# Weight splits of the A/B projections, issued two column blocks ahead and in front of the modulation steps

## The chip, the cores and the metric

The kernel runs on one core of a Trainium2 chip. A core has five engines, each working through its own list of instructions strictly in the written order: TensorE (PE in the profile; its weight loads are PEld) multiplies matrices into PSUM, VectorE (DVE) and ScalarE (ACT) do elementwise work, GpSimd (POOL) does elementwise work that does not touch PSUM, and SyncE (SP) only issues DMAs. An instruction that must wait for another engine or for a DMA holds back everything behind it on its own engine, DMA issues on SP included. The metric is device time in microseconds (us) of one execution; lower is better.

## The reference, cut to what matters

The program is a two-layer encoder trunk on 1024 tokens of width 1024, in fp32. Per layer:

```python
mod = silu(c) @ w_mod[l] + b_mod[l]            # six vectors of 1024, from a 1024 x 6144 matrix
h = rms_norm(x, g_attn[l]) * (1 + sc_a) + sh_a
proj = h @ w_in[l]                             # q, k, v of three head groups A, B, C
ya = neighborhood_attention(qa, ka, va, rpb_na[l])
yb = sliding_window_attention(qb, kb, vb, sink_sw[l], t5_table)
yc = axial_attention(qc, kc, vc, gq_ax[l], gk_ax[l])
y = concatenate([rms_norm(ya, ga), rms_norm(yb, gb), rms_norm(yc, gc)])
x = x + gt_a * (y @ w_o[l])
h = rms_norm(x, g_ffn[l]) * (1 + sc_f) + sh_f
gate, up = split(h @ w_gu[l])
x = x + gt_f * ((silu(gate) * up) @ w_down[l])
```

The change lies in `proj = h @ w_in[l]` and in the part of `mod` that is computed beside it.

## The kernel before, in words

**Split products.** TensorE multiplies in a short fp32 format. To keep fp32 precision, each operand is split in two tiles: a rounded copy `whi` (a CAST on ACT) and the rest `wlo` (a subtraction on DVE or POOL, which reads `whi` too). A product is then three matmuls (`mm3`): whi with hh, wlo with hh, whi with hl, where `hh` and `hl` are the split of h. So the first matmul of a product needs `whi`, and the second one needs `wlo`.

**The projection stage of a layer** has two parts.

*Part one* is a loop `for t in range(10)` over token blocks of 128 tokens. It projects, normalizes, rotates and transposes the C heads (`ps_c`, `cq`, `ct`, `qn`, `pq`, `pk`), and in its steps 2, 3, 6 and 7 it also runs the first two A/B column blocks (`ps_ab`): a column block `oc` is 128 columns of `w_in`, done in two halves of 512 tokens (`ab_proj(w, half)`, 24 matmuls each). Block 0 is done in steps 2 and 3, block 1 in steps 6 and 7. The split tiles of these two blocks share one pair of buffers (`"wx", 2`), so those of block 1 can be written only when the matmuls of block 0 are done. The V weights are loaded in step 4 (`v_stage`) and split in steps 6 and 7.

*Part two* first runs `for t in range(8)`: V of each token block (`v_proj`, product tile `ps_v`; token blocks 6 and 7 are done together by `v_proj(6, 7)`), the split of V by ACT and DVE (`v_split`, tile `vs`), one step of the bias tables of the A heads (`z_step`: load `zt`, subtract on POOL, store to `zAd`, three kinds of step in turn), and one modulation step (`mod_one`). Then `for oc in range(NE, 8)` with `NE = 2` runs the column blocks 2 to 7, each in two halves: the split of a coming block's weights, the product (`ps_ab`), the issue of a coming block's weight load, every fourth half a `mod_sum` (four matmuls into `ps_mod`), a `z_step`, up to two `mod_one`, and then the split of the product (`ab_split`: tile `qko`, first on ACT, then on DVE), whose store ACT issues one half later.

**A modulation step** `mod_one` is one load of 512 KB of `w_mod` on SP (tile `wmt`, three buffers) and one multiply-add on DVE (`acc`), which waits for that load. Eight steps make one of the six vectors; after the eighth, DVE splits the sum (`acch`, `accl`).

**Weight loads.** `w_ab(l, oc)` issues the load of a column block on SP into a staging tile `wst`. There are two staging buffers, and a third load can be issued only when both readers of the oldest one, the ACT cast and the subtraction, are done:

```python
    def stage():
        return wp.tile([P, 1024], F32, name="wst", tag="wst", bufs=2)
```

**PSUM.** The projections take their product tiles from eight banks, and in part two, after the V loop, from four of them. A product tile can be written only when the split that read the tile before it in that bank is done. In the built program, before and after the change alike, these are the first tiles of the column-block loop: in layer 0 the halves of block 2 take the banks of token blocks 5 and 6 of V, and in layer 1 the first half takes the bank of token block 7. The second tile of the first `mod_sum` takes the bank of block 2's first half, and the second half of block 3 that of block 2's second half: they wait for the `qko` of these halves on DVE.

**Order.** In part two all engines are pinned: each runs its instructions in the order of the Python code. In part one DVE, ACT and POOL are. The lines that set the order around the change are, in the V loop, `wab = split_tile(wst.pop(0), KC, eng=dve)` ahead of `v_split` of token block 6 (block 2's weights), and in the column-block loop the same line ahead of a block's first half (the next block's weights), with `wst.append(w_ab(l, oc + 2))` behind that half's product.

Of the kernel before, what the change touches and what calls it, by code (L numbers as in the profile page):

```python
# [22 lines left out]
KC = D // P  # L23
# [53 lines left out]
def f32(ap):  # L77
    return ap.bitcast(F32)
# [7 lines left out]
def trunk(ctx: ExitStack, tc, A, C, out):  # L86
    nc = tc.nc
    pe, act, dve, pool, sp = (
        Engine(tc, e) for e in (nc.tensor, nc.scalar, nc.vector, nc.gpsimd, nc.sync)
    )  # L90
# [5 lines left out]
    def open_pool(name, bufs=1, side="left", space=None):  # L96
        kw = dict(name=name, bufs=bufs, side=side, reuse_waits="tile")
        if space is not None:
            kw["space"] = space
            if space == PSUM:  # L100
                kw.pop("side")
        cm = tc.tile_pool(**kw)
        p = cm.__enter__()
        return cm, p
# [43 lines left out]
    def stage():  # L148
        return wp.tile([P, 1024], F32, name="wst", tag="wst", bufs=2)

    def parts(t, a):
        return t if a == 1 else t.rearrange("p (a b) -> p a b", a=a)

    def split_tile(st, a=1, hl=None, eng=None):
        pl, tag, bufs = hl or (wp, "whl", 8)
        hi = pl.tile([P, 1024], F32R, name="whi", tag=tag, bufs=bufs)
        lo = pl.tile([P, 1024], F32R, name="wlo", tag=tag, bufs=bufs)
        act.copy(hi, st)
        (eng or pool).tensor_tensor(out=lo, in0=st, in1=f32(hi), op=ALU.subtract)
        return parts(hi, a), parts(lo, a)  # L160
# [524 lines left out]
    def w_ab(l, oc):  # L685
        st = stage()
        c0 = oc * P if oc < 4 else 768 + (oc - 4) * P
        sp.dma_start(
            parts(st, KC), A["w_in"][l, :, c0 : c0 + P].rearrange("(k p) n -> p k n", p=P)
        )  # L690
        return st

    NE = 2
# [74 lines left out]
    wab = [w_ab(0, 0)]  # L768
# [41 lines left out]
    for l in range(2):  # L810
# [10 lines left out]
        ct_cm, ct = open_pool("ct", side="left")  # L821
# [7 lines left out]
        if l:  # L829
            wab = [w_ab(l, oc) for oc in range(NE)]  # L830
# [3 lines left out]
        def ab_proj(w, half):  # L834
            c = slice(half * H, (half + 1) * H)
            ps = psl.tile([P, 512], F32, name="ps_ab", tag="mm")
            for k in range(KC):
                mm3(ps, w[0][:, k], w[1][:, k], hh[:, k, c], hl[:, k, c], k == 0, k == 7)
            return ps

        def ab_split(oc, half, ps, pl):

            c = slice(half * H, (half + 1) * H)
            o = pl.tile([P, 2, H], F32R, name="qko", tag="qko", bufs=2)
            sc = -0.125 if oc in (0, 1, 4, 5, 6) else 1.0
            act.activation(o[:, 0, :], ps, AF.Copy, scale=sc)
            dve.scalar_tensor_tensor(
                out=o[:, 1, :], in0=ps, scalar=sc, in1=f32(o[:, 0, :]),
                op0=ALU.mult, op1=ALU.subtract,
            )  # L850

            def store(eng=sp):
                for j in range(2):
                    eng.dma_start(
                        qkd[oc, j, :, :, c].rearrange("z p t -> p z t"),
                        f32(o[j * 64 : j * 64 + 64]),
                    )

            return store
# [16 lines left out]
        def c_proj(*ts):  # L876
            psc.update(tokens_proj("ps_c", wC, ts))
# [7 lines left out]
        def c_split(t1):  # L885

            qn = ct.tile([P, 2, 5, 2, 64], F32R, name="qn", tag="qn", bufs=3)
            tq = t1[:, 0:6, :].rearrange("p (g h) d -> p g h d", g=2)
            tk = bc(t1[:, 6:8, None, :], [P, 2, 2, 64])
            act.copy(qn[:, :, 0:3, 0, :], tq)  # L890
            act.copy(qn[:, :, 3, :, :], tk)
            dve.tensor_tensor(
                out=qn[:, :, 0:3, 1, :], in0=tq, in1=f32(qn[:, :, 0:3, 0, :]), op=ALU.subtract
            )
            dve.tensor_tensor(
                out=qn[:, :, 4, :, :], in0=tk, in1=f32(qn[:, :, 3, :, :]), op=ALU.subtract
            )
            return qn
# [21 lines left out]
        def v_proj(*ts):  # L920
            psv.update(tokens_proj("ps_v", wV, ts))
# [23 lines left out]
        w = split_tile(wab.pop(0), KC, (ct, "wx", 2), dve)  # L945
# [7 lines left out]
        def v_stage(kp):  # L953
            if kp < 2:
                st = stage()
            elif kp == 2:
                st = ct.tile([P, 1024], F32, name="wsv")
            else:
                st = cp.tile([P, 1024], F32, name="wsv", tag="acc")
            for dst, v in w_in_src(l, V_COLS, kp)(parts(st, 2)):  # L960
                sp.dma_start(dst, v)
            vst.append(st)

        def v_split_w(eng):
            wV.append(split_tile(vst.pop(0), 2, eng=eng))
# [3 lines left out]
        for t in range(10):  # L969
            while abs_:  # L970
                ab_split(*abs_.pop(0), ct)()
            if t in (2, 3, 6, 7):
                abs_.append((t // 6, t % 2, ab_proj(w, t % 2)))
            elif t == 0:
                c_proj(4, 5)
            elif t in (4, 5):
                c_proj(t + 2)
            elif t > 7:
                v_proj(t - 8)
            if t == 7:  # L980
                v_split_w(dve)
                v_split_w(dve)
            if 0 < t < 8:
                qts[t] = next(norm[t])
            if t < 7:
                norm[t + 1] = c_norm(t + 1, psc[t + 1], ct_tile)
                next(norm[t + 1])
            if 0 < t < 9:
                qns[t - 1] = c_split(qts.pop(t - 1))
            if t > 1:  # L990
                c_turn(t - 2, qns.pop(t - 2))
            if t == 4:
                w = split_tile(wab.pop(0), KC, (ct, "wx", 2))
                for kp in range(4):
                    v_stage(kp)
            if t == 6:
                v_split_w(pool)
                v_split_w(dve)
            if l == 0 and t == 3:
                bias_rows()  # L1000
# [12 lines left out]
        wst = [w_ab(l, NE), w_ab(l, NE + 1)]  # L1013
# [32 lines left out]
        def z_step():  # L1046
            if z_steps:
                what, h = z_steps.pop(0)
                what(h)
# [5 lines left out]
        def mod_one():  # L1055
            l_, g = todo[0]
            k = going["step"]
            if k == 0:
                going["acc"] = cp.tile([P, 1024], F32, name="acc", tag="acc")
            acc = going["acc"]  # L1060
            mod_step(l_, g, k, acc, wm)
            going["step"] = (k + 1) % KC
            if k == KC - 1:
                todo.pop(0)
                hi, lo = (
                    wp.tile([P, 1024], F32R, name=f"acc{p}", tag="whl", bufs=8) for p in "hl"
                )
                dve.tensor_copy(hi, acc)
                dve.tensor_tensor(out=lo, in0=acc, in1=f32(hi), op=ALU.subtract)
                sums_due.append((l_, g, hi, lo))  # L1070
# [18 lines left out]
        for t in range(8):  # L1089
            if t == 4:  # L1090
                v_proj(4)
                v_proj(5)
            if t == 6:
                v_proj(6, 7)
                wab = split_tile(wst.pop(0), KC, eng=dve)
            v_split(t, psv[t])
            z_step()
            mod_one()

        store = None  # L1100
        close(ps_cm)
# [44 lines left out]
            return lambda: [divide(prs[c], rs, c) for c in range(2)]  # L1146

        for oc in range(NE, 8):
            w = wab
            for half in range(2):  # L1150
                if half == 0 and oc < 7:
                    wab = split_tile(wst.pop(0), KC, eng=dve)
                scored = early_scores() if oc == 7 else None
                ps = ab_proj(w, half)
                if store:
                    store(act)
                if scored:
                    scored()
                if half == 0 and oc < 6:
                    wst.append(w_ab(l, oc + 2))  # L1160
                i = 2 * (oc - NE) + half
                if i % 4 == 2:
                    mod_sum()
                z_step()
                for _ in range((2, 2, 2, 1, 2, 1, 2, 1, 2, 1, 0, 0)[i]):
                    mod_one()
                store = ab_split(oc, half, ps, ab)
# [421 lines left out]
        for n in range(-AHEAD - 1, N + 1):  # L1589
# [24 lines left out]
            if n == 54:  # L1614
                wst = [w_o_stage(k) for k in korder[:2]]
# [166 lines left out]
        for i, n in enumerate((6, 7, 0, 1, 2, 3, 4, 5)):  # L1782
            w = wc[i] if i < KC - NK else w_next()
# [403 lines left out]
        for u in range(NU):  # L2187
            i, t = divmod(u, NB)
# [25 lines left out]
            if t < NB - 1:  # L2214
                continue
            m, half = {
                1: (0, 0), 2: (0, 0), 6: (0, 1), 7: (1, 1), 4: (1, 0), 5: (1, 1), 3: (0, 1),
            }[num]
# [129 lines left out]
```

## Time and profile before

| What | Value |
|---|---|
| Median of three runs | 2460.08 us (2459.95 to 2464.16) |
| The profiled execution's own time | 2460.14 us |
| Its span, first to last instruction | 2458.4 us (1.7 us lie outside) |
| PE busy | 2387.5 us, 97% of the span |
| DVE, ACT, POOL busy | 74%, 50%, 31% of the span |
| Mean granted TensorE clock | 0.992 of full speed |
| Projection stage, layer 0 / layer 1 | about 84 to 250 us / 1286 to 1455 us |
| PE idle in 172 to 194 us (layer 0) | 2.8 us of 22 |
| PE idle in 1374 to 1387 us (layer 1) | 4.2 us of 13, granted clock there 0.74 |

PE is busy for nearly the whole span, so time is gained or lost where PE waits, or where its clock is lowered. The list of waits names, for each engine, who ended its waits; the timeline gives each instruction with its start, its duration, and in brackets the idle time of its engine ahead of it and what ended that. Matmuls overlap: one of 512 columns is recorded as 0.39 us long, but the next one starts 0.23 us later.

### The profile page before, as it was taken

What the parts mean: (1) busy time and instruction counts of PE and PEld (TensorE: products, weight loads), DVE (VectorE), ACT (ScalarE), POOL (GpSimd) and SP (SyncE); (2) the same over time, 40 slices, a digit from 0 to 9 for tenths busy, and PEclk for the clock granted to TensorE, in tenths of its full rate; (3) what the DMA queues carried; (4) which work ended last, traced back from release to release, by engine and by line L of the source; (5) the groups of instructions that cost most, each with busy time, mean ns of one, the idle gap of its engine ahead of it and who ended that gap; (6) DMA issues with size and microseconds to landing.
All of it is one profiled execution on the core that took longest, in us unless ns stands there. A gap on an engine that the chain in (4) does not pass through costs nothing.

```text
span 2458.4 us, 34300 instructions
## 1 busy us (share of the span) xinstructions
PE 2387.5 (97%) x12005; PEld 1991.2 (81%) x12005; DVE 1819.2 (74%) x2966; ACT 1227.1 (50%) x2306; POOL 764.6 (31%) x769
## 2 busy tenths in 40 slices
PE   8999999999999999999999999999999999999998
PEld 4787899878788787788787789987887888888886
DVE  5757999986967888586677679998688545446865
ACT  3422888954543333344543148888444343334443
POOL 1520445620244444300036124465004434430001
PEclk9999999999999999999999999999999999999999
DMA  8468205255245454596424851141624332229743
GB/s 285 149 188 282 56 6 145 57 165 160 86 142 173 158 178 152 163 274 193 152 85 116 279 165 27 48 148 50 206 86 141 119 121 95 99 96 296 209 134 110
DMA packets 285205, 356.04 MB, mean 145 GB/s; under 512 B 32996, under 2 KB 201532, under 8 KB 285032
## 3 DMA queue, kind: packets, MB, share of 16 engines
q1 hardware_dynamic: 277816, 341.12, 44.4%
q10 hardware_dynamic: 6912, 12.59, 1.6%
q8 instruction: 95, 1.56, 0.3%
q14 instruction: 78, 0.64, 0.1%
q0 software_dynamic: 304, 0.14, 0.0%
HBM read 269.62 MB, written 86.69 MB: 145 GB/s over the span
## 4 chain that ended last, share of the span: by engine, by line
PE 73%; DVE 9%; DMA 6%; issue 4%; ACT 4%; POOL 2%; SPq 1%; ACTq 0%; POOLq 0%; DVEq 0%
PE ps_w L49 28%; PE ps_d L49 14%; PE ps_o L49 7%; PE pv L49 6%; PE ps_ab L49 6%; PE T L49 4%; PE sC L49 3%; DMA wmt<-in_w_mod_dram 1%; SPq L49 1%; ACT pr L49 1%; DMA zAd<-zt 1%; PE sA L49 1%; DMA zt<-skA 1%; PE ps_v L49 1%; PE ps_c L49 1%
## 5 line engine op out<-in xcount | busy, mean ns | idle before, releaser
L49 PE MATMUL ps_d<-wpt 128*128 128x512 f32 x1848 | 424.3, 390 | 2.4 <-ACT wpt L49 2.1
L49 PEld LDWEIGHTS ps_d<-wpt 128*128 128x128 f32 x1848 | 345.6, 188 | 76.4 <-issue 3.0
L49 POOL TENSOR_SCALAR pr<-pr,rs 128x1024 f32<-128x1024 f32 (+4 forms) x252 | 206.9, 823 | 309.8 <-DVE rs L49 293.2
L49 POOL TENSOR_TENSOR sg<-sg,u 128x512 f32<-128x512 f32 x86 | 124.6, 1451 | 356.3 <-ACT sg L49 117.9
L49 PE MATMUL pv<-pt,vs 128*128 128x256 f32 x1216 | 202.0, 296 | 7.8 <-DVE rs L49 2.3
L49 DVE TENSOR_TENSOR pt<-T,pt 128x512 fp32r<-128x512 f32 x304 | 199.5, 680 | 11.4 <-ACT pt L49 9.9
L49 ACT CAST wpt<-w 128x512 fp32r<-128x512 f32 x154 | 95.7, 621 | 196.4 <-PE ps_d L49 175.1
L49 ACT CAST pt<-T 128x512 fp32r<-128x512 f32 x304 | 170.1, 586 | 43.3 <-PE T L49 41.7
L49 PE MATMUL T<-identr,pr 128*128 128x128 f32 x1288 | 187.0, 273 | 2.2 <-ACT rb L49 1.0
L49 PEld LDWEIGHTS pv<-pt,vs 128*128 128x128 f32 x1216 | 161.2, 189 | 23.0 <-DVE y L49 7.6
L49 DVE SCALAR_TENSOR_TENSOR acc<-wmt,condT,acc 128x512 f32<-128x512 f32 (+1 forms) x98 | 118.4, 1218 | 81.6 <-DMA wmt<-in_w_mod_dram 81.3
L49 DVE TENSOR_TENSOR wpt<-w,wpt 128x512 fp32r<-128x512 f32 x154 | 108.9, 707 | 84.4 <-ACT wpt L49 84.4
L49 ACT COPY u<-ps_w 128x512 f32<-128x512 f32 x128 | 75.1, 587 | 192.5 <-PE ps_w L49 192.4
L49 PEld LDWEIGHTS T<-identr,pr 128*128 128x128 f32 x1288 | 152.6, 140 | 22.0 <-issue 3.2
L49 POOL TENSOR_TENSOR wpt<-ws,wpt 128x512 fp32r<-128x512 f32 x80 | 112.8, 1410 | 180.3 <-ACT wpt L49 140.0
L49 ACT CAST wpt<-ws 128x512 fp32r<-128x512 f32 x176 | 107.8, 622 | 62.6 <-issue 28.4
L49 DVE TENSOR_TENSOR wpt<-ws,wpt 128x512 fp32r<-128x512 f32 x96 | 83.9, 885 | 59.0 <-ACT wpt L49 58.9
L49 DVE TENSOR_TENSOR wpt<-graw,wpt 128x512 fp32r<-128x512 f32 x154 | 110.0, 714 | 18.6 <-ACT wpt L49 18.5
L49 DVE TENSOR_REDUCE rs<-sC 128x1 f32<-128x1024 f32 x96 | 116.4, 1218 | 6.1 <-PE sC L49 5.7
L49 PE MATMUL ps_w<-h22h,wpt 128*128 128x512 f32 x352 | 111.7, 399 | 5.4 <-ACT sg L49 3.5
L49 DVE TENSOR_TENSOR ws<-wr 128x512 f32<-128x512 f32 x88 | 79.9, 910 | 48.6 <-POOL wpt L49 45.4
L49 ACT CAST whi<-wst 128x1024 fp32r<-128x1024 f32 x74 | 77.3, 1048 | 73.4 <-PE ps_o L49 47.9
(287 smaller groups left out, 6040.5 us busy)
## 6 DMA issues: line engine op xcount, KB each, us to landing
wr<-in_w_gu_dram SPq DMA_DIRECT2D x92, 512.0 KB, 4.2
gpd<-sg SPq DMA_DIRECT2D x154, 256.0 KB, 4.5
graw<-gpd SPq DMA_DIRECT2D x76, 512.0 KB, 3.7
w<-in_w_down_dram SPq DMA_DIRECT2D x110, 256.0 KB, 5.3
wmt<-in_w_mod_dram SPq DMA_DIRECT2D x48, 512.0 KB, 5.7
qk<-qkd SPq DMA_DIRECT2D x44, 512.0 KB, 7.2
wst<-in_w_o_dram SPq DMA_DIRECT2D x32, 512.0 KB, 3.5
wmt<-in_w_mod_dram SPq DMA_DIRECT2D x64, 256.0 KB, 3.6
```

The costliest lines, as they stand in the source:

```text
L49: ins = op(*args, **kwargs)
```

## The change

Three edits, the same in both layers.

1. *Part one, step 4:* the split of block 1's weights is issued at the head of the step, in front of the step's C work, and its subtraction runs on DVE; before, it stood at the end of the step and ran on POOL.
2. *V loop, step 6:* in front of the split of token block 6, the weights of block 2 and those of block 3 are split; behind each split stand the load of the block two further on (4 and 5) and one modulation step. The modulation steps of the loop's steps 5 and 6 are left out in exchange, so that there are still eight.
3. *Column-block loop:* a split made in block `oc` is that of block `oc + 2`, and the load issued is that of block `oc + 4`; before, it was `oc + 1` and `oc + 2`.

No instruction is added or removed; in each layer one subtraction moves from POOL to DVE.

```diff
@@ for t in range(10): @@
             while abs_:
                 ab_split(*abs_.pop(0), ct)()
+            if t == 4:
+                w = split_tile(wab.pop(0), KC, (ct, "wx", 2), dve)
             if t in (2, 3, 6, 7):
                 abs_.append((t // 6, t % 2, ab_proj(w, t % 2)))
...
             if t == 4:
-                w = split_tile(wab.pop(0), KC, (ct, "wx", 2))
                 for kp in range(4):
                     v_stage(kp)
@@ for t in range(8): @@
             if t == 6:
                 v_proj(6, 7)
-                wab = split_tile(wst.pop(0), KC, eng=dve)
+                wabs = []
+                for oc in range(NE, NE + 2):
+                    wabs.append(split_tile(wst.pop(0), KC, eng=dve))
+                    wst.append(w_ab(l, oc + 2))
+                    mod_one()
             v_split(t, psv[t])
             z_step()
-            mod_one()
+            if t not in (5, 6):
+                mod_one()
@@ for oc in range(NE, 8): @@
-            w = wab
+            w = wabs.pop(0)
             for half in range(2):
-                if half == 0 and oc < 7:
-                    wab = split_tile(wst.pop(0), KC, eng=dve)
+                if half == 0 and oc < 6:
+                    wabs.append(split_tile(wst.pop(0), KC, eng=dve))
                 scored = early_scores() if oc == 7 else None
                 ps = ab_proj(w, half)
...
-                if half == 0 and oc < 6:
-                    wst.append(w_ab(l, oc + 2))
+                if half == 0 and oc < 4:
+                    wst.append(w_ab(l, oc + 4))
```

What this does to the order on an engine is shown at three places, as differences of the built programs (- before, + after). First VectorE in the V loop of layer 0, from the fifth modulation step on (`acc` is a modulation step, `vs` the split of a V token block, `wlo` the subtraction of a weight split):

```order
 L49 SCALAR_TENSOR_TENSOR acc<-wmt,condT,acc 128x1024
 L49 TENSOR_TENSOR vs<-ps_v,vs 128x8x64
+L49 TENSOR_TENSOR wlo<-wst,whi 128x1024
 L49 SCALAR_TENSOR_TENSOR acc<-wmt,condT,acc 128x1024
 L49 TENSOR_TENSOR wlo<-wst,whi 128x1024
-L49 TENSOR_TENSOR vs<-ps_v,vs 128x8x64
 L49 SCALAR_TENSOR_TENSOR acc<-wmt,condT,acc 128x1024
-L49 TENSOR_TENSOR vs<-ps_v,vs 128x8x64
+L49 TENSOR_TENSOR vs<-ps_v,vs 128x8x64 x2
 L49 SCALAR_TENSOR_TENSOR acc<-wmt,condT,acc 128x1024
```

The two `wlo` (blocks 2 and 3) now stand in front of the sixth and of the seventh modulation step, and the V splits of token blocks 6 and 7 both stand behind the seventh; before, that of token block 6 stood in front of it.

Second, SyncE at the same place (`wst` is the load of a column block's weights, `wmt` that of a modulation step, `zt` and `zAd` belong to the bias tables):

```order
 L49 DMA zAd<-zt 128x576
+L49 DMA wst<-in_w_in_dram 128x8x128
+L49 DMA wmt<-in_w_mod_dram 128x1024
+L49 DMA wst<-in_w_in_dram 128x8x128
 L49 DMA wmt<-in_w_mod_dram 128x1024
 L49 DMA zt<-skA_91 64x14x64 x2
-L49 DMA wmt<-in_w_mod_dram 128x1024
 L49 DMA zAd<-zt 128x896
```

The loads of blocks 4 and 5 now stand in front of the sixth and of the seventh modulation load, and both of those in front of the load of a bias table.

Third, VectorE in part one of layer 0, around the head of step 4 (`qko` is the split of a column block's product, `qn` that of the C heads):

```order
 L49 SCALAR_TENSOR_TENSOR qko<-ps_ab,qko 128x512
+L49 TENSOR_TENSOR wlo<-wst,whi 128x1024
 L49 RECIPROCAL r_861<-r_861 128x8
 L49 TENSOR_TENSOR cq<-ps_c,r_861 128x512
 L49 TENSOR_TENSOR cq<-cq,g_411 128x512
```

The subtraction of block 1's weights now stands on VectorE in front of the C work of step 4; on GpSimd it stood behind that of the step.

## The prediction

> **What bounds the kernel now.** I read the page first, then the list of PE's waits in the two projection stages, then the timelines of PE, DVE, SP and POOL around each wait. The page says that PE sets the time:
>
> ```profile
> span 2458.4 us, 34300 instructions
> PE 2387.5 (97%) x12005; PEld 1991.2 (81%) x12005; DVE 1819.2 (74%) x2966; ACT 1227.1 (50%) x2306; POOL 764.6 (31%) x769
> ```
>
> So an edit counts only by the waits that it takes from PE or gives to it. Waits of PE in the projections (total, times, longest), the first row from 80 to 260 us (layer 0), the two behind the "..." from 1280 to 1470 us (layer 1):
>
> ```profile
> PE ps_ab L49 <- POOL wlo L49: 0.4, 1, 0.4
> ...
> PE ps_ab L49 <- DVE vs L49: 4.2, 1, 4.2
> PE ps_ab L49 <- POOL wlo L49: 1.6, 1, 1.6
> ```
>
> Layer 0 has two more, of 1.1 and 1.6 us, whose rows follow below: about 9 us in all. The longest one is dearer than it looks. PE in layer 1, at the first half of block 2:
>
> ```profile
> 1373.91 0.39 PE L49 MATMUL ps_v<-wlo,hh 128*128 128x512 f32 x1
> 1378.50 0.80 PE L49 MATMUL ps_ab<-hh,whi 128*128 128x512 f32 x1 [4.20 <-DVE vs L49]
> ...
> 1383.24 0.40 PE L49 MATMUL ps_ab<-hl,whi 128*128 128x512 f32 x1
> ```
>
> Eleven matmuls between the second and the last row take 4.74 us where eleven at 0.227 us take 2.5: after this pause PE runs slower at first and loses 2.2 us more. The page of the Trainium skill "TensorE: Matmul & The Clock Gate" (Part 1: The HAM clock gate) has the rule: after an idle window of about 3.4 us the clock is halved until PE has been busy for as long. The trace agrees (0.43 against 0.23 us); I charge the 2.2 us of the rows.
>
> That first half waits for the last V split of token block 7 (`vs`), whose PSUM bank it takes. DVE there in layer 1:
>
> ```profile
> 1369.63 0.68 DVE L49 TENSOR_TENSOR vs<-ps_v,vs 128x512 fp32r<-128x512 f32 x1
> 1372.16 1.28 DVE L49 SCALAR_TENSOR_TENSOR acc<-wmt,condT,acc 128x1024 f32<-128x1024 f32 x1 [1.85 <-DMA wmt<-in_w_mod_dram]
> 1373.36 1.22 DVE L49 TENSOR_TENSOR wlo<-wst,whi 128x1024 fp32r<-128x1024 f32 x1
> ...
> 1375.73 2.11 DVE L49 SCALAR_TENSOR_TENSOR acc<-wmt,condT,acc 128x1024 f32<-128x1024 f32 x1 [0.55 <-DMA wmt<-in_w_mod_dram]
> 1377.77 0.68 DVE L49 TENSOR_TENSOR vs<-ps_v,vs 128x512 fp32r<-128x512 f32 x1
> 1382.02 1.28 DVE L49 SCALAR_TENSOR_TENSOR acc<-wmt,condT,acc 128x1024 f32<-128x1024 f32 x1 [3.58 <-DMA wmt<-in_w_mod_dram]
> ...
> 1385.21 1.22 DVE L49 TENSOR_TENSOR wlo<-wst,whi 128x1024 fp32r<-128x1024 f32 x1
> ```
>
> The V split stands behind the seventh modulation step (1375.73), and that one waits for its load. So the landing of modulation loads sets this stretch, and with it SP, which issues them. SP, and POOL's bias step that SP waits for:
>
> ```profile
> 1367.30 0.38 SPq L49 DMA_DIRECT2D wmt<-in_w_mod_dram  x1
> 1369.16 1.29 SPq L49 DMA_DIRECT2D zt<-skA  x2
> 1370.54 1.18 SPq L49 DMA_DIRECT2D wmt<-in_w_mod_dram  x1
> 1374.68 2.08 POOL L49 TENSOR_TENSOR zt<-mA,zt 128x896 f32<-128x896 f32 x1 [7.83 <-DMA zt<-skA]
> 1377.21 0.38 SPq L49 DMA_DIRECT2D wmt<-in_w_mod_dram  x1
> 1377.65 0.63 SPq L49 DMA_DIRECT2D wst<-in_w_in_dram  x1
> ```
>
> From issue to the multiply-add that waited for it a modulation load takes 4.9 us (1367.30 to 1372.16), or 5.2 us where other loads go just ahead (1370.54 to 1375.73). Note the last row: the weight load of block 4 is issued behind the eighth modulation load, when its staging buffer has long been free. It holds nobody up.
>
> **The change, part by part.**
>
> *Edit 1* ends the two waits for POOL's `wlo`: a gain of 0.4 + 1.6 = 2.0 us. DVE gets 1.22 us, and with the wait for ACT's cast some 2.3 us, in front of the C work of step 4, which PE needs only a step later; I count nothing for that. If that cover is gone, one step comes up to 2.3 us late in each layer, 4.6 us in all.
>
> *Edit 2* gives `wlo` of block 3 early: that ends layer 0's wait for it (1.1 us; with the lost overlap 1.3). But look at the load that now follows each split. Only two staging buffers exist, and both are full. So SP can issue the load of block 4 only when DVE has done `wlo` of block 2, and that of block 5 only when DVE has done `wlo` of block 3. In SP's list the sixth modulation load stands behind the first of these, the seventh behind the second. And on DVE `wlo` of block 3 stands behind the sixth modulation step. That closes a ring: DVE waits for a modulation load, SP cannot issue the next one until DVE has done a `wlo`, and DVE does it only after the modulation step. Loads that were issued ahead are now issued one by one. Queued behind on DVE: both V splits, for which PE waits.
>
> Layer 1, from the rows above. The V split at 1369.63 is untouched and ends at 1370.3. `wlo` of block 2 follows at once and ends at 1371.45 (starts 1.2 us apart); SP issues block 4 (0.63 us) and at 1372.1 the sixth modulation load, which before went out at 1367.30. It lands 5.2 us later, 1377.3; the multiply-add and `wlo` of block 3 take 2.4 us: 1379.7. SP issues block 5 and at 1380.35 the seventh load; it lands at 1385.55; multiply-add 1.2, two V splits 0.6 and 0.68: 1388.05. PE starts block 2 at 1388.1, not 1378.5: **9.6 us**, with the same slow start as before.
>
> It goes on behind. SP issues the bias loads at 1380.8; POOL starts 5.5 us after their issue (1369.16 to 1374.68) and takes 2.1: 1388.4; then SP issues the eighth modulation load at 1388.8, which lands at 1393.7 (4.9). From that step's multiply-add to the end of the next `wlo` the rows show 4.4 us (1382.02 to 1386.43): 1398.1. Only then may SP issue block 6 (0.63), a bias store (0.4) and, at 1399.1, the next modulation load: it lands at 1404.3, the one behind it has landed when DVE comes to it, and after two multiply-adds of 1.2 and the split `qko` of block 2's first half DVE is at 1407.5. PE has by then done three halves: 7.7 us for the slow first one, twice 5.44 (24 matmuls), and two matmuls of `mod_sum`: 1407.1. **0.4 us** wait. The second half's `qko` comes behind two more modulation steps, the later load of which needs the buffer that was read at 1405.5: it lands some 5 us later, 1410.5, and with 1.2 and 0.68 `qko` ends at 1412.4, where PE wants to go on at 1408.0: **4.4 us**, and 2.2 for the clock. Layer 1: 9.6 + 0.4 + 4.4 + 2.2 = 16.6.
>
> Layer 0 in the same way from its own rows (DVE, then PE):
>
> ```profile
> 167.98 0.68 DVE L49 TENSOR_TENSOR vs<-ps_v,vs 128x512 fp32r<-128x512 f32 x1
> ...
> 178.21 0.39 PE L49 MATMUL ps_ab<-hh,whi 128*128 128x512 f32 x1
> ...
> 185.18 0.50 PE L49 MATMUL ps_ab<-hh,wlo 128*128 128x512 f32 x1 [1.14 <-DVE wlo L49]
> ...
> 193.26 0.50 PE L49 MATMUL ps_ab<-hh,whi 128*128 128x512 f32 x1 [1.64 <-DVE qko L49]
> ```
>
> Here it is block 2's second half (178.21) that takes the bank of a V block, token block 6. Its split was done long ahead; now it stands behind the seventh modulation step. The same chain from 168.66: sixth load issued 170.4, `wlo` of block 3 done 178.0, seventh load landed 183.85, multiply-add and one V split 185.7. PE waits 7.5 us and loses 2.2 by the clock. Then bias loads 179.1, POOL done 186.7, eighth load 187.1 to 192.0, next `wlo` 196.4, next modulation load 197.4 to 202.6, first `qko` 205.7; PE arrives at 193.45 + 5.44 + 0.46 = 199.35 and waits 6.35 us. The second `qko` ends at 210.7. So the matmul that started at 193.26 starts at 210.75: **17.5 us** later, waits of before already in it, and 2.2 for the clock: 19.7.
>
> *Edit 3* alone moves a `wlo` half a block earlier or later in a stretch (194 to 250 us) where PE waits for nothing; nothing.
>
> Sum: 19.7 + 16.6 - 2.0 = **34.3 us slower**. Against the profiled execution's own 2460.14 us (its span and 1.7 us around it), which lies 0.06 us from the median, this is **2494 us**. After the third block the delay stays: PE has nine more halves of 5.44 us there, enough to cover the modulation loads that come later.
>
> *Bounds of the landing time.* Ten landings stand in these chains, five in a layer. The shortest and the longest modulation load of the layer 1 stage that DVE waited for:
>
> ```profile
> 1353.51 0.42 SPq L49 DMA_DIRECT2D wmt<-in_w_mod_dram  x1
> ...
> 1385.62 1.84 SPq L49 DMA_DIRECT2D wmt<-in_w_mod_dram  x2
> ...
> 1357.82 1.28 DVE L49 SCALAR_TENSOR_TENSOR acc<-wmt,condT,acc 128x1024 f32<-128x1024 f32 x1 [0.55 <-DMA wmt<-in_w_mod_dram]
> ...
> 1391.87 3.50 DVE L49 SCALAR_TENSOR_TENSOR acc<-wmt,condT,acc 128x1024 f32<-128x1024 f32 x2 [2.72 <-DMA wmt<-in_w_mod_dram]
> ```
>
> 4.3 us and 6.25 us: 0.9 less or about 1 more than I take, so 25 us or 44 us. I take 5.2, the row with other loads just ahead, since a weight load of the same size now goes ahead of each. The page "DMA: Bandwidth & Descriptors" of the Trainium skill (Anatomy of one DMA, a fit for POOL's queue) gives 2.0 us plus the bytes by 436 GB/s, by my estimate 3.2 us for 512 KB; by it the sum would be 15 us, 2475 us. No row of this kernel's modulation loads is that short.
>
> **The rivals.** *A: the ring, as above*, 2494 us; for it the two staging buffers and the order on SP and DVE. *B: the ring, but cheap.* SP held back leaves the DMA engines to fewer loads, so that each lands in 4.3 us, and the later pauses stay too short to lower the clock: 2494 - 9 - 4 = 2481 us. Against it: a weight load goes ahead of each modulation load, and the pauses that I find are of 4 us and more. The page's fit named above is the far end of this rival, 2475 us. *C: the other side, faster.* The modulation loads come as early as before and the splits just move up: all waits listed go, 2.0 + 1.3 + 1.6 + 4.2 + 2.2 = 11 us, 2449 us. It decides if SP is not held at the first `wst`, that is if the subtraction of block 2 were done by 1367.3, when SP comes to it. The V split ahead of it on DVE ends only at 1370.3. *D: no change:* what is won at POOL, at `wlo` and at `vs` pays for a shorter ring, 2460 us; that needs landings of about 2 us.
>
> **How the numbers follow.** A 0.72, B 0.18, C 0.06, D 0.04. The time is A's, 2494 us. The range 2479 to 2507 holds A and B with the bounds of the landing and the uncounted 4.6 us of edit 1. About 0.2% (5 us) is what a measurement of this kernel can tell from no change: slower by more 0.90, within 0.04, faster by more 0.06.
>
> **What would show it.** In the list of PE's waits: no POOL `wlo` any more; in layer 0 a new wait of 6 to 9 us for DVE `vs` at block 2's second half, in layer 1 that wait grown to about 14 us; new waits of 4 to 7 us for `qko` at the first `mod_sum` or just behind it; more stretches of half clock. On SP, idle time ahead of each `wst` up to the end of a `wlo` on DVE, and modulation loads one by one. I am wrong if SP issues the sixth modulation load near 167 and 1368 us, or if PE's first wait for `vs` is shorter than 4.2 us.

## The result, and the profile after

The changed kernel is **slower**: 2504.4 us (median of four runs, 2499.42 to 2507.12) against 2460.0 us for the kernel before, a ratio of 1.0169 (95% interval 1.0155 to 1.0184), or 44.4 us. The forecast was 2494 us, range 2479 to 2507. Its profiled execution took 2499.42 us, the shortest of the four, at a mean granted clock of 0.986 (0.992 before), so the traces explain 39 us of the 44: the spans are 2458.4 and 2497.6 us. The other three runs took 5 to 8 us longer at 0.982 to 0.984; they have no trace, and where these 5 us of the median lie stays open.

The first two lines of the profile after:

```profile
span 2497.6 us, 34295 instructions
PE 2393.6 (96%) x12005; PEld 1994.0 (80%) x12005; DVE 1815.4 (73%) x2968; ACT 1226.7 (49%) x2306; POOL 758.3 (30%) x767
```

PE does the same 12005 matmuls and is busy only 6 us longer; the other 33 us of the span are idle time. PE's four longest waits in each projection stage of the changed kernel (total, times, longest; above the "..." from 80 to 270 us, layer 0, below it from 1290 to 1500 us, layer 1):

```profile
PE ps_ab L49 <- DVE vs L49: 9.8, 1, 9.8
PE ps_mod L49 <- DVE qko L49: 7.4, 1, 7.4
PE ps_ab L49 <- DVE qko L49: 4.6, 1, 4.6
PE ps_v L49 <- POOL wlo L49: 0.2, 1, 0.2
...
PE ps_ab L49 <- DVE vs L49: 12.3, 1, 12.3
PE ps_ab L49 <- DVE qko L49: 4.8, 1, 4.8
PE ps_mod L49 <- DVE qko L49: 2.1, 1, 2.1
PE ps_v L49 <- POOL wlo L49: 1.5, 1, 1.5
```

These are the waits that the prediction named, at its places: `vs` at block 2, then `qko` at the first `mod_sum` and behind it. No `ps_ab` waits for POOL's `wlo` any more, but there is one wait that no step foresaw: in layer 1 PE now waits 1.5 us for POOL's `wlo` at `ps_v`, a split of the V weights.

Who holds DVE shows in its timeline (start, duration, instruction, in brackets the idle time ahead of it and what ended it), layer 0:

```profile
169.41 1.22 DVE L49 TENSOR_TENSOR wlo<-wst,whi 128x1024 fp32r<-128x1024 f32 x1
178.12 1.29 DVE L49 SCALAR_TENSOR_TENSOR acc<-wmt,condT,acc 128x1024 f32<-128x1024 f32 x1 [7.50 <-DMA wmt<-in_w_mod_dram]
179.33 1.22 DVE L49 TENSOR_TENSOR wlo<-wst,whi 128x1024 fp32r<-128x1024 f32 x1
186.85 1.28 DVE L49 SCALAR_TENSOR_TENSOR acc<-wmt,condT,acc 128x1024 f32<-128x1024 f32 x1 [6.31 <-DMA wmt<-in_w_mod_dram]
188.05 1.28 DVE L49 TENSOR_TENSOR vs<-ps_v,vs 128x512 fp32r<-128x512 f32 x2
195.54 1.28 DVE L49 SCALAR_TENSOR_TENSOR acc<-wmt,condT,acc 128x1024 f32<-128x1024 f32 x1 [6.20 <-DMA wmt<-in_w_mod_dram]
...
198.73 1.22 DVE L49 TENSOR_TENSOR wlo<-wst,whi 128x1024 fp32r<-128x1024 f32 x1
206.41 0.75 DVE L49 TENSOR_SCALAR acc<-wmt,condT 128x1024 f32<-128x1024 f32 x1 [6.47 <-DMA wmt<-in_w_mod_dram]
```

And SP's issues in the same stretch of the changed kernel:

```profile
170.65 0.38 SPq L49 DMA_DIRECT2D wst<-in_w_in_dram  x1
171.07 0.58 SPq L49 DMA_DIRECT2D wmt<-in_w_mod_dram  x1
180.57 0.38 SPq L49 DMA_DIRECT2D wst<-in_w_in_dram  x1
181.00 0.58 SPq L49 DMA_DIRECT2D wmt<-in_w_mod_dram  x1
181.67 1.35 SPq L49 DMA_DIRECT2D zt<-skA  x2
191.01 0.33 SPq L49 DMA_DIRECT2D zAd<-zt  x1
191.38 0.43 SPq L49 DMA_DIRECT2D wmt<-in_w_mod_dram  x1
199.97 0.38 SPq L49 DMA_DIRECT2D wst<-in_w_in_dram  x1
200.45 0.53 SPq L49 DMA_DIRECT2D zAd<-zt  x1
201.03 0.95 SPq L49 DMA_DIRECT2D wmt<-in_w_mod_dram  x2
```

Read the two lists crosswise: a `wlo` ends (170.63), SP issues `wst` (170.65) and then `wmt` (171.07), which lands; DVE does `acc` (178.12) and the next `wlo` (179.33, done at 180.55), and SP issues the next `wst` (180.57). Three links of this kind follow each other. Each of DVE's four idle stretches above is 6 us or more, and each ends with a modulation load. While this goes on, the DMA engines are less busy than before. The view of windows gives for the changed kernel (length, busy time and instructions of PE, PEld, DVE, ACT, POOL, granted clock, DMA share, GB/s)

```profile
172.00:212.00 40.00, 21.78 (x83) 16.64 (x81) 11.88 (x12) 3.66 (x6) 4.45 (x4) 0.80 0.59 173
```

and for a stretch of the kernel before with as many matmuls (83)

```profile
172.00:194.00 22.00, 19.21 (x83) 15.14 (x82) 15.39 (x15) 3.77 (x6) 4.54 (x4) 1.00 0.88 278
```

The share of 0.59 in place of 0.88 is a mean over stretches that are full and stretches that are empty. Two slices of the changed kernel, one ahead of the second pair of loads and one in which it is moved:

```profile
178.00:180.00 2.00, 0.97 (x5) 0.47 (x3) 1.88 (x2) 0.60 (x1) 0.00 (x0) 1.00 0.00 0
182.00:184.00 2.00, 0.00 (x0) 0.00 (x0) 0.00 (x0) 0.00 (x0) 0.00 (x0) 0.66 0.98 300
```

From 176 to 182 us the DMA engines have next to nothing to do (0.00 to 0.05 in slices of 2 us), and then they are full (0.98 to 1.12 by the view's count, from 182 to 188 us). The empty slices are the loss: the loads are issued too late.

### The profile page after: what moved, and what is told of

It reads as the page before. It is cut to its first block, busy times and chain, and to the rows that moved or that the text cites. A ratio compares the mean times of both kernels' runs of the same rounds, so it can differ in the third digit from the quotient of the medians.

```text
span 2497.6 us, 34295 instructions
## 1 busy us (share of the span) xinstructions
PE 2393.6 (96%) x12005; PEld 1994.0 (80%) x12005; DVE 1815.4 (73%) x2968; ACT 1226.7 (49%) x2306; POOL 758.3 (30%) x767
## 4 chain that ended last, share of the span: by engine, by line
PE 72%; DVE 10%; DMA 6%; issue 4%; ACT 4%; POOL 2%; SPq 1%; ACTq 0%; POOLq 0%; DVEq 0%
PE ps_w L49 29%; PE ps_d L49 13%; PE ps_o L49 7%; PE pv L49 5%; PE T L49 4%; PE ps_ab L49 4%; PE sC L49 3%; DMA wmt<-in_w_mod_dram 2%; PE ps_c L49 1%; ACT pr L49 1%; DMA zt<-skA 1%; PE sA L49 1%; PE ps_v L49 1%; SPq L49 1%; DMA zAd<-zt 1%
## 5 line engine op out<-in xcount | busy, mean ns | idle before, releaser
L49 PE MATMUL ps_ab<-hh,whi 128*128 128x512 f32 x256 | 104.2, 407 | 32.0 <-DVE vs L49 22.1
L49 ACT CAST wpt<-graw 128x512 fp32r<-128x512 f32 x154 | 94.9, 616 | 43.9 <-DMA graw<-gpd 38.8
```

The costliest lines, as they stand in the source:

```text
L49: ins = op(*args, **kwargs)
```

## The experiments

All times below are medians in us, each compared with runs of the kernel before on the same chip (medians of 2460.0 to 2461.5 us). The column "SP waits for wlo" is the sum of SP's waits for DVE's `wlo` in 160 to 212 us and 1360 to 1430 us, from the list of waits of each kernel.

| Kernel | Time | Ratio to before (95%) | SP waits for wlo |
|---|---|---|---|
| before | 2460.0 | 1 | 4.3 |
| after | 2504.4 | 1.0169 (1.0155 to 1.0184) | 40.2 |
| edit 1 alone | 2461.0 | 1.0001 (0.9991 to 1.0011) | 4.1 |
| after, loads of blocks 4 and 5 put back | 2478.1 | 1.0067 (1.0049 to 1.0085) | 22.7 |
| before, with one link of the ring | 2473.8 | 1.0048 (1.0030 to 1.0066) | 15.5 |
| after, small loads for blocks 4 and 5 | 2498.3 | 1.0151 (1.0135 to 1.0167) | 37.6 |
| after, no ring | 2469.1 | 1.0032 (1.0021 to 1.0043) | 0.2 |
| no ring, product splits first | 2464.1 | 1.0012 (1.0003 to 1.0022) | 0.3 |
| before, product splits first | 2455.9 | 0.9979 (0.9969 to 0.9989) | 1.9 |
| the same, and block 3's split first | 2455.4 | 0.9981 (0.9973 to 0.9990) | 1.4 |

### Edit 1 alone

```diff
+            if t == 4:
+                w = split_tile(wab.pop(0), KC, (ct, "wx", 2), dve)
...
             if t == 4:
-                w = split_tile(wab.pop(0), KC, (ct, "wx", 2))
```

> Edit 1 alone: the split of block 1's weights at the head of step 4, its subtraction on VectorE; everything else as before. My theory (the loss is the ring of VectorE and SyncE, which edit 1 has no part in): 2458 to 2460 us. PE's waits for POOL wlo of 0.4 us (layer 0) and 1.6 us (layer 1) at ps_ab go; but the kernel after the change shows a wait of 1.5 us for POOL wlo at ps_v in layer 1 that was not there before, so of the 2.0 us of the prediction I now expect about 0.5 us. The rival, that edit 1's 2.3 us on VectorE ahead of the C work of step 4 are not covered: up to 4.6 us slower, 2465 us, with new waits of PE for VectorE in the C work.

Measured: 2461.0 us, ratio 1.0001. The interval reaches from 2.2 us faster to 2.7 us slower, so the rival's 4.6 us is out, and a gain of 2.0 us is not shown either. The median lies 1 us past the expected 2460 us, but 0.5 us below that of the kernel before on the same chip, 2461.5 us: the expected gain of about 0.5 us is too small for these runs to show or to refute. PE's waits tell why a gain would be small (layer 1):

```profile
PE ps_ab L49 <- DVE vs L49: 3.0, 1, 3.0
...
PE ps_v L49 <- POOL wlo L49: 0.9, 1, 0.9
```

The 1.6 us for POOL's `wlo` at `ps_ab` are gone, 0.9 us of it is back at `ps_v`. PE comes sooner to the next product and waits there for the next split on POOL. In layer 0 PE's wait for `qko` is 2.1 us, where the kernel before had 1.64.

### The loads of blocks 4 and 5 put back

```diff
                     wabs.append(split_tile(wst.pop(0), KC, eng=dve))
-                    wst.append(w_ab(l, oc + 2))
                     mod_one()
...
             if t not in (5, 6):
                 mod_one()
+            if t == 7:
+                wst += [w_ab(l, 4), w_ab(l, 5)]
```

> The changed kernel with one thing put back: the loads of blocks 4 and 5 are issued behind the eighth modulation load, and no longer in front of the sixth and the seventh. The order on VectorE, PE, ScalarE and GpSimd is that of the changed kernel. Ring theory: SyncE issues the sixth and seventh modulation loads without waiting for a wlo (near 167 and 1368 us), PE's wait for vs at block 2 goes in layer 0 (from 9.8 us) and falls to 5 us or less in layer 1 (from 12.3 us). A rest stays, since edit 3 puts the split of block 4 at the head of block 2, where its load has only just been issued: 4 to 8 us of waits for qko in a layer. Sum 2472 to 2484 us. The rival that the order on VectorE alone is the cause (both V splits stand behind two subtractions and two modulation steps, whatever SyncE does): no better than 2497 us, with the wait for vs of 9 us and more still there. The rival that a weight load just ahead makes each modulation load late by traffic: the waits shrink here too, to about the same time; the run with small weight loads tells it from the ring.

Measured: 2478.1 us. PE's waits, layer 0 and, below the "...", layer 1:

```profile
PE ps_mod L49 <- DVE qko L49: 5.6, 1, 5.6
PE ps_ab L49 <- DVE qko L49: 4.4, 1, 4.4
...
PE ps_ab L49 <- DVE qko L49: 4.9, 1, 4.9
PE ps_ab L49 <- DVE vs L49: 2.6, 1, 2.6
```

The wait for `vs` went from 9.8 us to nothing and from 12.3 to 2.6 us, with VectorE's order untouched; order alone as the cause is out for that wait. The time is in the range of the ring theory, but in layer 0 more is left than the 4 to 8 us of waits for `qko` that were expected (5.6 + 4.4 = 10.0 us; in layer 1 4.9 us and 1.9 us more at `ps_mod`), and my reason for the rest was wrong. I had it that the split of block 4 would wait for its own load. SP shows something else:

```profile
177.39 0.38 SPq L49 DMA_DIRECT2D wmt<-in_w_mod_dram  x1
177.82 9.03 SPq L49 DMA_DIRECT2D wst<-in_w_in_dram  x3
186.95 0.53 SPq L49 DMA_DIRECT2D zAd<-zt  x1
187.52 0.94 SPq L49 DMA_DIRECT2D wmt<-in_w_mod_dram  x2
```

The group of three `wst` lasts 9 us, up to 186.85: the third is the load of block 6, which needs the `wlo` of block 4, and that one ends on DVE at 186.46. The ring's third link, from edit 3, was still in place, with two modulation loads behind it.

### One link of the ring, in the kernel before

```diff
             if t == 6:
                 v_proj(6, 7)
                 wab = split_tile(wst.pop(0), KC, eng=dve)
+                wst.append(w_ab(l, 4))
...
-                if half == 0 and oc < 6:
+                if half == 0 and 2 < oc < 6:
                     wst.append(w_ab(l, oc + 2))
```

> The kernel before with one link of the ring alone: the load of block 4 is issued right behind the split of block 2, so in front of the seventh modulation load, and not in the column-block loop. VectorE's order is that of before. Ring theory: SyncE can issue that load only when the wlo of block 2 is done (172.8 and 1374.6 us), the seventh modulation load goes out 5 to 6 us later than before, in layer 1 the V split behind it and with it PE's first matmul of block 2 come 5 us later (a wait for vs of 9 us, not 4.2), in layer 0 the wlo of block 3, behind the eighth step, comes some 7 us late. Sum about 12 to 14 us: 2470 to 2476 us. Rivals: the order on VectorE is the cause: nothing changes, 2460 us. Traffic: one weight load moves in front of one modulation load in each layer, 1 to 2 us each: 2461 to 2464 us.

Measured: 2473.8 us, ratio 1.0048, some 12 us slower than before by one moved line in each layer. PE's longest waits, layer 0 and layer 1:

```profile
PE ps_ab L49 <- DVE wlo L49: 8.1, 1, 8.1
...
PE ps_ab L49 <- DVE vs L49: 9.6, 1, 9.6
```

Both as the ring theory had them (7 and 9 us), and neither rival gives them: VectorE's order is that of before, and traffic was priced at 1 to 4 us.

### Small loads for blocks 4 and 5

```diff
...
+        if oc in (4, 5):
+            v = parts(st, KC)[:, 0:1]
+            sp.dma_start(v, src[:, 0:1])
+            return v
...
```

The kernel leaves out seven eighths of these two blocks' weights; the split repeats the eighth that is there.

> The changed kernel with the loads of blocks 4 and 5 cut to an eighth (64 KB in place of 512 KB; the split repeats that eighth, so these two blocks are left uncomputed, while every engine has the same instructions of the same sizes in the same order). The waits of SyncE for the staging buffers stay, the traffic goes. Ring theory: SyncE is held as before, and the four landings behind these loads come at most 1 us sooner each: 2496 to 2502 us, with a wait for vs of 8 us and more in layer 0 and 10 us and more in layer 1. Traffic as the cause: the modulation loads behind the small loads land in about 4 us or less and most of the loss goes: 2480 us or less.

Measured: 2498.3 us, ratio 1.0151. SP is still held, and the loss stays. One expectation failed: the wait for `vs` in layer 0 is 5.9 us, where 8 us and more were expected (10.4 us in layer 1, as expected), since all four landings came sooner by more than the 1 us allowed, the first one by 1.9 us. What the traffic is worth can be read by comparing the time from SP's issue to the multiply-add. In this kernel, layer 1 (SP, then DVE):

```profile
1394.35 0.43 SPq L49 DMA_DIRECT2D wmt<-in_w_mod_dram  x1
...
1401.09 0.43 SPq L49 DMA_DIRECT2D wmt<-in_w_mod_dram  x1
...
1398.27 1.28 DVE L49 SCALAR_TENSOR_TENSOR acc<-wmt,condT,acc 128x1024 f32<-128x1024 f32 x1 [4.32 <-DMA wmt<-in_w_mod_dram]
...
1405.30 1.28 DVE L49 SCALAR_TENSOR_TENSOR acc<-wmt,condT,acc 128x1024 f32<-128x1024 f32 x1 [4.62 <-DMA wmt<-in_w_mod_dram]
```

3.9 and 4.2 us; behind a full weight load, in the changed kernel, 5.0 and 5.4. In layer 0 the same two are 5.1 and 4.4 here, 7.05 and 5.85 there. The four differences (1.9, 1.5, 1.1 and 1.2 us) add to 5.6 us. In the two traces PE gains about that in the two projection stages (3.6 and 3.0 us), and the medians are 6 us apart; the two traced spans differ by only 1.9 us (2497.6 and 2495.7), since this execution was slower elsewhere. Traffic sets the size of a link, not its existence.

### The ring taken out

```diff
             if t not in (5, 6):
                 mod_one()
+            if t == 7:
+                wst += [w_ab(l, 4), w_ab(l, 5)]
...
-                if half == 0 and oc < 4:
-                    wst.append(w_ab(l, oc + 4))
+                if half == 0 and 2 < oc < 5:
+                    wst.append(w_ab(l, oc + 3))
```

> The changed kernel with all four weight loads placed so that SyncE need not wait for a subtraction: blocks 4 and 5 behind the eighth modulation load, blocks 6 and 7 behind the first half of blocks 3 and 4. The order on PE, VectorE, ScalarE and GpSimd is that of the changed kernel, the split of block 4 at the head of block 2 included. In the run with the loads of blocks 4 and 5 put back, SyncE still stood 9 us in each layer at the third load, that of block 6, which needs the wlo of block 4, with two modulation loads behind it. Ring theory: that is the rest of the loss, so 2462 to 2470 us here, with the wait for qko at the first mod_sum 3 us or less (5.6 us there) and SyncE idle nowhere up to the end of a wlo. The rival, that the rest comes from VectorE's order (the subtraction of block 4 and two modulation steps in front of qko): 2475 to 2482 us, as in that run.

Measured: 2469.1 us, ratio 1.0032. SP's waits for `wlo` in layer 0, in the changed kernel:

```profile
SPq L49 <- DVE wlo L49: 21.0, 3, 8.9
```

and in this one:

```profile
SPq L49 <- DVE wlo L49: 0.2, 1, 0.2
```

With every instruction of PE, VectorE, ScalarE and GpSimd in the changed kernel's order, and four DMA issues per layer moved on SP, 35 of the 44 us are gone. That is what the places of these four issues cost: the ring, and in it the weight load in front of a modulation load, which the run before puts at about 6 us. Some 9 us stay, as a wait for `qko` of 5.1 us in layer 0 and 5.0 us in layer 1 (the second half of block 3), where the kernel before had 1.64 and none. DVE ahead of it in layer 0:

```profile
183.82 1.22 DVE L49 TENSOR_TENSOR wlo<-wst,whi 128x1024 fp32r<-128x1024 f32 x1
...
188.94 0.69 DVE L49 SCALAR_TENSOR_TENSOR qko<-ps_ab,qko 128x512 fp32r<-128x512 f32 x1
192.05 1.39 DVE L49 SCALAR_TENSOR_TENSOR acc<-wmt,condT,acc 128x1024 f32<-128x1024 f32 x1 [2.42 <-DMA wmt<-in_w_mod_dram]
193.60 1.28 DVE L49 SCALAR_TENSOR_TENSOR acc<-wmt,condT,acc 128x1024 f32<-128x1024 f32 x1 [0.16 <-DMA wmt<-in_w_mod_dram]
194.80 0.68 DVE L49 SCALAR_TENSOR_TENSOR qko<-ps_ab,qko 128x512 fp32r<-128x512 f32 x1
```

The second `qko` stands behind two modulation steps that wait for their loads. Here VectorE's order does count, though little beside the ring.

### The ring taken out, and product splits first

```diff
                     wabs.append(split_tile(wst.pop(0), KC, eng=dve))
+                    v_split(oc + 4, psv[oc + 4])
                     mod_one()
-            v_split(t, psv[t])
+            if t < 6:
+                v_split(t, psv[t])
...
+                store = ab_split(oc, half, ps, ab)
                 for _ in range((2, 2, 2, 1, 2, 1, 2, 1, 2, 1, 0, 0)[i]):
                     mod_one()
-                store = ab_split(oc, half, ps, ab)
```

> The kernel with the ring taken out (all three edits, the four weight loads where SyncE needn't wait) is still 8 us slower than before, and has a wait for qko of 5 us at the second half of block 3 in each layer. Here it gets the splits of products in front of the modulation steps too: each V split right behind a weight split, each qko in front of its block's modulation steps. If the two modulation steps in front of the second qko are the rest: the waits for qko fall to 3 us or less, no half clock follows, and the time is 2456 to 2463 us. If it is the subtraction of block 4 at the head of block 2, which stands behind the eighth modulation step and in front of the first qko, whatever follows: 2465 us or more, with the wait moved to the first qko.

Measured: 2464.1 us, ratio 1.0012, 1 us past the range given for "the two modulation steps are the rest". The waits for `qko` are down to 0.2 us, so that reading of them holds; 6 of the 9 us are back. The remainder are two other waits of PE (layer 0, layer 1):

```profile
PE ps_ab L49 <- DVE own L49: 2.8, 1, 2.8
...
PE ps_ab L49 <- DVE vs L49: 3.0, 1, 3.0
```

`own` reads the result of `mod_sum`; in layer 0 it now stands behind two modulation steps that wait for their loads (3.24 and 0.91 us) and a `wlo`. Even without the ring, then, the conversions two blocks ahead bring no gain here.

### Product splits first, without any of the edits

```diff
-            v_split(t, psv[t])
+            if t < 7:
+                v_split(t, psv[t])
+            if t == 6:
+                v_split(7, psv[7])
...
+                store = ab_split(oc, half, ps, ab)
                 for _ in range((2, 2, 2, 1, 2, 1, 2, 1, 2, 1, 0, 0)[i]):
                     mod_one()
-                store = ab_split(oc, half, ps, ab)
```

> The kernel before, without any of the three edits, with the splits of products moved in front of the modulation steps: that of token block 7 of V right behind that of token block 6 (in front of the seventh modulation step), and in the column-block loop each qko in front of the block's modulation steps. Nothing is moved past anything on SyncE but ScalarE's and VectorE's own work. If the landing of modulation loads ahead of a split sets PE's waits, as the prediction reads them: the wait for vs in layer 1 falls from 4.2 us to 1.5 us or less with no half clock behind it, and the wait for qko in layer 0 goes: 4 to 7 us in all, 2453 to 2456 us. If the modulation steps, now later, hold back something else (the eighth step, and with it the wlo of block 3): 2459 to 2462 us.

Measured: 2455.9 us, ratio 0.9979. In layer 1 the wait for `vs` is down from 4.2 to 1.4 us:

```profile
PE ps_ab L49 <- POOL wlo L49: 1.7, 1, 1.7
PE ps_ab L49 <- DVE vs L49: 1.4, 1, 1.4
```

and the wait for `qko` in layer 0 is gone. So the reading of these two waits of the kernel before is right: a PSUM bank that PE waits for was freed late because its split stood behind a modulation load.

The last kernel moves block 3's weight split too, in front of the eighth modulation step, with the loads where the kernel before has them:

```diff
             z_step()
+            if t == 7:
+                wabs.append(split_tile(wst.pop(0), KC, eng=dve))
             mod_one()
...
-                if half == 0 and oc < 7:
-                    wab = split_tile(wst.pop(0), KC, eng=dve)
+                if half == 0 and 2 < oc < 7:
+                    wabs.append(split_tile(wst.pop(0), KC, eng=dve))
```

> The same with the split of block 3's weights moved too, in front of the eighth modulation step; the weight loads stay where the kernel before has them, so SyncE waits for no subtraction. This is what edit 2 was after (block 3's subtraction early), without its loads. The wait for wlo of block 3 in layer 0 (1.1 us) goes as well: 1 us less than with the splits of products alone, 2452 to 2455 us. If SyncE is held after all (the load of block 5 or the modulation loads later than before): 2460 us or more.

Measured: 2455.4 us, ratio 0.9981, 0.4 us past the expected range and not to be told from the one without it. PE's wait for `wlo` in layer 0 is gone as expected, so the place was right; a gain of 1 us is not shown, it is below what these runs resolve. Both kernels beat the one before by 4 to 5 us, about the 0.2% that a measurement can tell, with intervals that leave out 1.

A third and a fourth staging buffer, which would take away what SP waits for with the loads left where the change puts them, were not tried.

## Why the prediction was right, and where it missed

**The bound and the ring: right.** PE's waits decide; SP is held at each `wst` up to the end of a `wlo` (170.63 and 170.65 us above); the sixth and seventh modulation loads go out one by one; the V splits are late, and then the first two `qko`. Taking the ring out returned 35 of 44 us, and putting one link in cost 12. The forecast lies 10 us under the median and the range holds it. Rival C (faster) fell with SP's sixth modulation load, issued at 171.07 and not near 167 us. Rival D (no change) needed landings of about 2 us; none in these chains took less than 4.2 us.

**The sizes.** Each wait against the step of the prediction that priced it:

| Place | Predicted us | Measured us |
|---|---|---|
| Layer 0, `vs` at block 2's second half | 7.5 | 9.8 |
| Layer 0, `qko` at the first `mod_sum` | 6.35 | 7.4 |
| Layer 0, second `qko` (210.75 less 206.2) | 4.5 | 4.6 |
| Layer 1, `vs` at block 2 (4.2 + 9.6) | 13.8 | 12.3 |
| Layer 1, `qko` at the first `mod_sum` | 0.4 | 2.1 |
| Layer 1, second `qko` | 4.4 | 4.8 |
| Edit 1, `ps_ab` waits for POOL | -2.0 | -2.0, and +1.7 at `ps_v` |

The measured column is higher by 5.8 us; with that the sum of 34.3 would be 40.1, against 39.2 us between the two spans. Against the signs that the prediction gave, 9.8 and 7.4 us are above their ranges (6 to 9, 4 to 7), and 2.1 us is below.

*The landing of 5.2 us* was too small in layer 0. From the issue to the multiply-add the sixth load took 7.05 us (171.07 to 178.12) and the seventh 5.85 (181.00 to 186.85): 2.5 us more than two landings of 5.2, which is the 2.3 us by which the wait for `vs` was missed; 7.05 us is also past the longest landing that the bounds allowed, 6.25. In layer 1 the same two took 5.0 and 5.4 us, as I had it, and the chain from the last untouched V split to PE's start was 0.5 us shorter than the sum had it (17.3 us, not 17.8). The rest of the 1.5 us by which that wait came out shorter lies ahead of the chain: against the kernel before, this V split is 20.3 us later (1369.63 and 1389.93), but PE's last matmul of V 21.35 us (1373.91 and 1395.26).

*The bias step's 5.5 us* from the issue of its loads to POOL's start was mis-sized too. POOL in the changed kernel, layer 0:

```profile
188.88 2.10 POOL L49 TENSOR_TENSOR zt<-mA,zt 128x896 f32<-128x896 f32 x1 [22.67 <-DMA zt<-skA]
```

Issued at 181.67, it is 7.2 us (6.8 in layer 1, 1400.72 to 1407.49). The eighth modulation load behind it landed sooner than taken, in 4.2 us (191.38 to 195.54), not 4.9, which took part of this error out again.

*Edit 1* is the step that failed as a mechanism: "a gain of 0.4 + 1.6 = 2.0 us". I looked for its cover only on VectorE (and that held: nothing was lost there) and not at what PE meets next. PE runs into the next split on POOL, `ps_v`, 1.5 us in layer 1 and 0.2 in layer 0.

*The clock* was charged well. Behind the wait of 9.8 us nine matmuls take 4.0 us where nine at 0.227 take 2.0, behind the second `qko` ten take 4.4 us, not 2.3: together 4.1 us in layer 0, where I had twice 2.2.

*Rival B* (fewer loads in flight, so that each lands in 4.3 us) went the wrong way: only the eighth load, with no weight load in front, came in at 4.2 us, and the loads behind a weight load took about what was priced (layer 1) or longer (layer 0). With 64 KB in front in place of 512 KB, the four took 3.9 to 5.1 us, behind 512 KB 5.0 to 7.05. The fit of the Trainium skill on which its far end hung ("DMA: Bandwidth & Descriptors", Anatomy of one DMA, for GpSimd's queue; by my estimate 3.2 us for 512 KB) is not borne out for these loads, which SP issues, by any row here: the shortest of the eight is 3.9 us.

## What to carry to other kernels

A load that is issued earlier is no gain if its buffer is still being read: in-order issue then turns the buffer's reader into a gate for every load behind it, here three gates of some 20 us together in each layer, for loads that nobody needed yet. Before moving a load up, find the instruction that frees its buffer, and check that nothing urgent stands behind the load on its queue, nor that freeing instruction behind something that this queue brings. What did pay, a little, was to put the instructions that free PSUM for PE in front of the ones that wait for DMA, and to move no load at all.

## What the runs showed of the hardware that was not expected

A 512 KB modulation load issued right behind a 512 KB weight load took 5.0 to 7.05 us to its use; behind a 64 KB load it took 3.9 to 5.1 us. So the load in front cost 1.1 to 1.9 us, although the mean DMA share of this stretch is only 0.59. The mean misleads here: while the two pairs of layer 0 are moved (173.0 to 175.0 and 182.5 to 185.0 us, in slices of half a microsecond) the share is 0.96 to 1.28, at 311 to 436 GB/s, and in between it is near nothing. At these rates the 448 KB that the small load leaves out are 1.1 to 1.5 us, an estimate from these slices that fits three of the four differences.

The first pair in layer 0 was slower than the three others both with the full load in front (7.05 us) and with the small one (5.1 us). The trace shows where the time went: from 175.5 to 177.5 us the share is 0.06 to 0.09, about one of the 16 DMA engines, and the multiply-add starts only at 178.12. With the small load there is such a tail too (0.04 to 0.13 from 175.0 to 176.5 us). In both traces one 16 KB packet of the instruction queue, of about 1 us, was moved among the loads of this pair, and none among those of the three others. That this packet held up the one engine is likely, but no run here shows it.
